# Merging two dilated attention outputs: the factors by transposed statistics and a spreading transfer in place of small copies and TensorE transposes

## The chip, the cores and the metric

The kernel runs on one core of one Trainium2 chip. The metric is the device time of one execution in microseconds (us). Beside the time of an execution stands its span in the profile, from the first to the last instruction.

Engine names are those of the profile: PE is TensorE's matmul (PEld its weight load), DVE is VectorE, ACT is ScalarE, POOL is GpSimd, SP is SyncE, whose queue issues nearly all transfers.

## The reference

One encoder block on 1024 positions of width 1024: a normalised and modulated input is projected to q, k, v of two attentions (A dilated, B neighbourhood) and to gates; both attentions are projected, gated, added; a ConvFFN follows. The change is in attention A. It has 8 heads of width 64 and three patterns of the same q, k, v, whose results are merged by their softmax denominators:

```python
DIL_PATTERNS = ((128, 1), (512, 4), (2048, 16))

def mixture_of_dilations(q, k, v, rel_bias):
    outs, lses = [], []
    for window, dilation in DIL_PATTERNS:
        o, lse = dilated_window_attention(q, k, v, rel_bias, window, dilation)
        outs.append(o)
        lses.append(lse)                       # lse = m + log(l), the row maximum and the sum of exponentials
    w = jax.nn.softmax(jnp.stack(lses, axis=0), axis=0)
    return jnp.einsum('gbsh,gbshd->bshd', w, jnp.stack(outs, axis=0))
```

## The kernel before

Everything is kept transposed: channels on the partitions, positions along the free dimension, in an order in which the four residues modulo 4 stand in blocks of 256 ("r"). Products are made of three float32r matmuls each (L84 to L86: high by high, high by low, low by high), with operands split into a high and a low part.

**The mixers' stage.** From about 157 to 655 us the attentions run in 101 slots, written out by hand. In each slot some steps of attention are interleaved with `fill` steps, which are the remaining projections (L84 to L86, or L365): one step is one k of such a product, a job has sixteen. The order of PE, DVE and ACT in this stage is the order of the program text (`manual_schedule`). POOL and SP are not in that list: a planner with a timeline of its own places their instructions, and once placed, each queue runs strictly in order on the chip. The projections' weights are loaded by `w_load` (L65), two buffers deep, and split by ACT (L638, high part) and POOL (L639, low part) one job ahead; a load waits until the split of the job before has freed its buffer.

**A dilated head** takes 16 score tiles: in slots s0 to s0+3 the "far" ones (patterns 2 and 3 together, one residue r at a time), in s0+4 to s0+7 the "near" ones (pattern 1, blocks b of 128 positions). DVE adds the bias and takes the negative maximum, ACT takes the exponential and its sum (`softmax`, L579). Both go into a column of the tile `st`: 128 partitions, heads i of the pair, statistic (near maximum, near sum, far maximum, far sum), 8 columns. Two slots later PE transposes the probabilities into a PSUM tile T (L703 far, L749 near), ACT and DVE split it (L588, L589), one slot later PE multiplies by v (L715, L766), and ACT and DVE bring the result to the tiles u1 (near) and u23 (far): 128 partitions = two heads of 64 channels, 1024 positions, not yet divided by anything. PSUM holds two T tiles.

**The merge** is made for each of the four pairs of heads (`DilPair`, s0 = 16 times the pair). Near and far statistics lie in different orders over the partitions: near has partition = (r, j) and column = block b, far has partition = (q, j) with 32 j, and column = 2r + g. Before the change:

- `exchange` (L799): sixteen DVE copies of 32 partitions a pair, in slots s0+13 to s0+16, bring the far statistics into near order (xs).
- `factors` (s0+16) and `shares` (s0+17): a few DVE operations on 128 x 16 and one exponential on ACT give the two factors, near and far, for every position.
- `give` (L825): sixteen DVE copies a pair bring the far factor back into far order (fx).
- `spread` (L830, POOL): one factor column is repeated over 64 columns, for four blocks and two heads at once: fw, 128 x 512. `weigh` (L838, L840): PE transposes fw in four pieces into a T tile, which so holds the factor on all 64 channel partitions of its head, and DVE multiplies 512 columns of u by it. Four times a pair: near and far, two halves.
- `merge` (L847, POOL): u23 plus u1, reordered; the result goes to DRAM (L848, `oa`) and is read in the stage behind the mixers.

After the four pairs come the eight heads of attention B in slots 64 to 100. The last pair's merge falls into their first slots.

Of the kernel before, what the change touches and what calls it, by code (L numbers as in the profile page):

```python
# [17 lines left out]
S = 1024  # L18
# [11 lines left out]
def hybrid_encoder(tc, xT, c, w_ada, small, w_in, p1_bias, p23_bias, na_bias, ln2_mult, ident, w_br, w_out,  # L30
# [198 lines left out]

    vb_c = dram.tile([S, 512], FT, name="vbc")  # L230
    g_scr = dram.tile([16, 128, S], FT, name="gs")
    o_scr = [dram.tile([4, 128, S], FT, name=n) for n in ("oa", "ob")]
    v_scr = dram.tile([S + 9 * 128, 512], FT, name="v")
    va_s, va_b = v_scr[:S], v_scr[S:].rearrange("(j p) n -> j p n", j=9)
# [413 lines left out]
    class DilHead:  # L648
# [32 lines left out]
        def far_scores(self, r):  # L681
            qs, ks, kl, qb = qks[self.pr]
            ensure(qk_marks[self.pr])
            i, st = self.i, self.st()
            s = ps_l.tile([128, 512], FT, name="S")
            P = self.P[r] = sm_pool.tile([128, 2, 256], FT, name="P", bufs=5)
            for g in range(2):
                d = s[:, 256 * g:256 * g + 256]
                qc = slice(256 * r + 128 * g, 256 * r + 128 * g + 128)
                kc = slice(256 * r, 256 * r + 256)  # L690
                pe.matmul(d, qs[i][:, qc], ks[i][:, kc], start=True, stop=False)
                pe.matmul(d, qs[i][:, qc], kl[i][:, kc], start=False, stop=True)  # L692
            for g in range(2):
                d = s[:, 256 * g:256 * g + 256]
                e = 2 * r + g
                softmax(d, self.bt[:, 640 - 128 * g:896 - 128 * g], P[:, g], st[:, i, 2, e:e + 1], st[:, i, 3, e:e + 1])

        def far_turn(self, r):
            P = self.P.pop(r)
# [20 lines left out]
        def near_scores(self, n):  # L720
            qs, ks, kl, qb = qks[self.pr]
            ensure(qk_marks[self.pr])
            i, st = self.i, self.st()
            s = ps_l.tile([128, 512], FT, name="S")
            P = sm_pool.tile([128, 2, 256], FT, name="P", bufs=5)
            for x_ in range(2):
                b = 2 * n + x_
                t0, t1 = block_chunks(b)[0]
                d = s[:, 256 * x_:256 * x_ + 256]
                mid = t0 is not None and t1 is not None  # L730
                for dd, *keys in [(d, t0, 2)] if mid else [(d[:, 0:128], t0), (d[:, 128:256], t1)]:
                    pe.matmul(dd, qb[i][:, 128 * b:128 * b + 128], window(ks[i], *keys), start=True, stop=False)
                    pe.matmul(dd, qb[i][:, 128 * b:128 * b + 128], window(kl[i], *keys), start=False, stop=True)
            for x_ in range(2):
                b = 2 * n + x_
                off = block_chunks(b)[1]
                softmax(s[:, 256 * x_:256 * x_ + 256], self.bt[:, off:off + 256], P[:, x_], st[:, i, 0, b:b + 1],
                        st[:, i, 1, b:b + 1])
                self.P["near", b] = P[:, x_]

        def near_turn(self, js):
# [31 lines left out]
    class DilPair:  # L773
        def __init__(self, pr):
            self.pr, s0 = pr, 16 * pr
            at(s0, "first", self.begin) if pr else self.begin()
            for i in range(2):
                DilHead(self, pr, i, s0 + 8 * i, lambda: self.u, lambda: self.st)
            for r in range(4):
                at(s0 + 13 + r, "first", self.exchange, r)  # L780
                at(s0 + 18 + r, "first", self.give, r)
            at(s0 + 16, "last", self.factors)
            at(s0 + 17, "last", self.shares)
            for n, (g, z) in enumerate(((0, 0), (0, 1), (1, 0), (1, 1))):
                s = s0 + 18 + n + g
                at(s, "last", self.spread, g, z)
                at(s + 2, "W", self.weigh, g, z)
            at(s0 + 25, "first", self.merge)

        def begin(self):  # L790
            self.u = [at_pool.tile([128, S], FT, name=n) for n in ("u1", "u23")]
            self.st = sm_pool.tile([128, 2, 4, 8], FT, name="st")
            self.fw = {}

        def exchange(self, r):
            if r == 0:
                self.xs = at_pool.tile([128, 2, 2, 8], FT, name="xs")
            for q in range(4):
                dve.tensor_copy(self.xs[32 * r:32 * r + 32, :, :, q:8:4],  # L799
                                self.st[32 * q:32 * q + 32, :, 2:4, 2 * r:2 * r + 2])  # L800

        def factors(self):
            st, xs = self.st, self.xs
            fa = at_pool.tile([128, 2, 2, 8], FT, name="fa")
            fb = at_pool.tile([128, 2, 2, 8], FT, name="fb", bufs=1)
            fl = at_pool.tile([128, 2, 8], FT, name="fl", bufs=1)
            dve.tensor_tensor(fl, st[:, :, 0], xs[:, :, 0], OP.min)
            dve.tensor_tensor(fa[:, 0], fl, st[:, :, 0], OP.subtract)
            dve.tensor_tensor(fa[:, 1], fl, xs[:, :, 0], OP.subtract)
            act.activation(fa, fa, AF.Exp)  # L810
            self.fa, self.fb, self.fl = fa, fb, fl

        def shares(self):
            st, xs, fa, fb, fl = self.st, self.xs, self.fa, self.fb, self.fl
            dve.tensor_tensor(fb[:, 0], fa[:, 0], st[:, :, 1], OP.mult)
            dve.tensor_tensor(fb[:, 1], fa[:, 1], xs[:, :, 1], OP.mult)
            dve.tensor_tensor(fl, fb[:, 0], fb[:, 1], OP.add)
            dve.reciprocal(fl, fl)
            for g in range(2):
                dve.tensor_tensor(fa[:, g], fa[:, g], fl, OP.mult)  # L820
            self.fac = [fa[:, 0], at_pool.tile([128, 2, 8], FT, name="fx")]

        def give(self, r):
            for q in range(4):
                dve.tensor_copy(self.fac[1][32 * q:32 * q + 32, :, 2 * r:2 * r + 2],  # L825
                                self.fa[32 * r:32 * r + 32, 1, :, q:8:4])

        def spread(self, g, z):
            fw = self.fw[g, z] = at_pool.tile([128, 4, 2, 64], FT, name="fw")
            pool.tensor_scalar(fw, self.fac[g][:, :, 4 * z:4 * z + 4].rearrange("p i b -> p b i")  # L830
                               .rearrange("p b (i o) -> p b i o", o=1).to_broadcast([128, 4, 2, 64]), 1.0, None, OP.mult)

        def weigh(self, g, z):
            fw = self.fw.pop((g, z))
            ensure(self.done)
            pt = ps_a.tile([128, 512], FT, name="T")
            for b in range(4):
                pe.transpose(pt[:, 128 * b:128 * b + 128], fw[:, b], idt)  # L838
            dst = self.u[g][:, 512 * z:512 * z + 512]
            return lambda: dve.tensor_tensor(dst, dst, pt, OP.mult)  # L840

        def merge(self):
            u = self.u
# [882 lines left out]
```

## Time and profile before

| | |
|---|---|
| time, median of 3 runs | 1537.97 us (1537.17 to 1539.8) |
| profiled execution: time | 1539.41 us |
| profiled execution: span | 1537.3 us |
| mean granted TensorE clock | 0.988 |
| PE busy over the span | 1499.0 us (98%) |
| DVE, ACT, POOL busy | 996.0, 770.4, 775.8 us (65%, 50%, 50%) |
| DMA: moved, share of 16 engines (queue q1) | 205.24 MB in all, 41.1% |

How its lines are read: a group's line names the source line, the engine, the operation, the tiles written and read, the shape and the count; then its busy time in us and the mean ns of one; then the idle time of the engine just before them and what ended it. A line of the timeline names the start in us, the duration in us, the engine, the line, and in brackets the idle time before it. A line of the table by stage has the stretch, then for PE, PEld, DVE, ACT and POOL the busy time with the number of instructions, the granted clock, the DMA share and GB/s. A line of DMA issues ends with the median us from issue to landing. A line of the waits has the total us waited, how often, and the longest. Matmuls are pipelined and their ends are modelled, so the distance from start to start says more than the durations.

### The profile page before, as it was taken

The page shows a single profiled execution, that of the slowest core. Times are in us where ns is not written, and L with a number is a line of the kernel's source. Part 1 is how long each engine was busy: PE and PEld are TensorE (multiplying, and loading weights), DVE is VectorE, ACT ScalarE, POOL GpSimd, SP SyncE. Part 2 cuts the span into 40 slices and gives each one's busy share as a digit, 9 for nine tenths or more (in the row PEclk, how much of TensorE's full clock was granted, in tenths as well). Part 3 has the DMA queues.
Part 4 walks back from the last instruction along what each step waited for, and adds up shares of the span by engine and source line. Part 5 has one row for each costly group of instructions (what it writes and reads, how often), then busy time and mean ns, then how long its engine had stood idle before and what let it go on. Part 6 is the DMA issues. An engine that isn't in the chain of part 4 may idle for free. (4 is left out here: it accounts for less than half of the span.)

```text
span 1537.3 us, 21792 instructions
## 1 busy us (share of the span) xinstructions
PE 1499.0 (98%) x7740; PEld 1270.1 (83%) x7740; DVE 996.0 (65%) x1892; ACT 770.4 (50%) x1437; POOL 775.8 (50%) x640
## 2 busy tenths in 40 slices
PE   8999999999999999999999899999999998999997
PEld 7988888889798998878888677888888887878787
DVE  6675357575656655645525888876666667786765
ACT  4331566666656566643345454444444447475542
POOL 1021344443335444512267668776777765779721
PEclk8999999999999999999999999999999999999999
DMA  9567333333625456577644112222222224523323
GB/s 352 187 240 258 94 106 81 108 91 104 185 82 153 127 140 171 154 241 232 213 141 154 62 62 96 90 82 83 82 82 85 87 79 162 193 75 124 117 55 110
DMA packets 112436, 205.24 MB, mean 134 GB/s; under 512 B 40484, under 2 KB 53156, under 8 KB 112292
## 3 DMA queue, kind: packets, MB, share of 16 engines
q1 hardware_dynamic: 112056, 203.59, 41.1%
q8 instruction: 61, 1.00, 0.3%
q14 instruction: 47, 0.39, 0.1%
q10 hardware_dynamic: 272, 0.26, 0.1%
HBM read 158.73 MB, written 42.47 MB: 131 GB/s over the span
## 5 line engine op out<-in xcount | busy, mean ns | idle before, releaser
L61 POOL TENSOR_TENSOR wlo<-wraw,whi 128x512 fp32r<-128x512 f32 (+1 forms) x96 | 118.3, 1253 | 172.9 <-ACT whi L57 139.1
L84 PE MATMUL pj<-h,whi 128*128 128x512 f32 x448 | 187.7, 419 | 1.8 <-ACT h L207 1.4
L85 PE MATMUL pj<-h,whi 128*128 128x512 f32 x448 | 177.8, 397 | 1.6 <-DVE h L209 1.6
L86 PE MATMUL pj<-h,wlo 128*128 128x512 f32 x448 | 177.2, 396 | 0.0
L61 POOL TENSOR_TENSOR wsl<-big,wsh 128x512 fp32r<-128x512 f32 (+1 forms) x90 | 123.6, 1395 | 47.7 <-ACT wsh L57 47.7
L639 POOL TENSOR_TENSOR wlo<-wraw,whi 128x512 fp32r<-128x512 f32 x58 | 74.9, 1301 | 117.2 <-ACT whi L638 117.2
L589 DVE TENSOR_TENSOR tl<-T,th 128x512 fp32r<-128x512 f32 (+3 forms) x120 | 77.1, 653 | 72.9 <-ACT th L588 71.4
L1384 DVE SCALAR_TENSOR_TENSOR big<-wc,sm,big 128x256 f32<-128x256 f32 (+1 forms) x132 | 106.9, 859 | 16.1 <-ACT big L1378 15.9
L581 ACT ACTIVATE P<-P,st 128x256 f32<-128x256 f32 x128 | 64.1, 502 | 95.9 <-DVE st L580 95.9
L86 PEld LDWEIGHTS pj<-h,wlo 128*128 128x128 f32 x448 | 85.0, 190 | 18.9
L84 PEld LDWEIGHTS pj<-h,whi 128*128 128x128 f32 x448 | 85.6, 191 | 13.6 <-ACT h L207 1.9
L85 PEld LDWEIGHTS pj<-h,whi 128*128 128x128 f32 x448 | 85.6, 191 | 13.2 <-DVE h L209 3.0
L57 ACT ACTIVATE whi<-wraw 128x1024 fp32r<-128x1024 f32 (+2 forms) x52 | 50.7, 975 | 73.0 <-PE pj L85 27.6
L1384 DVE SCALAR_TENSOR_TENSOR big<-pj,sm,big 128x512 f32<-128x512 f32 x132 | 67.0, 563 | 17.6 <-ACT big L1378 17.6
L61 POOL TENSOR_TENSOR wsl<-wraw,wsh 128x384 fp32r<-128x384 f32 (+1 forms) x46 | 54.4, 1204 | 44.6 <-ACT wsh L57 44.4
L910 POOL TENSOR_SCALAR P<-P,stb 128x288 f32<-128x288 f32 (+1 forms) x32 | 40.2, 1257 | 72.1 <-DVE stb L907 64.7
L588 ACT ACTIVATE th<-T 128x512 fp32r<-128x512 f32 (+3 forms) x120 | 65.6, 566 | 20.3 <-PE T L919 14.0
L1378 ACT ACTIVATE big<-wc,sm 128x512 f32<-128x512 f32 x44 | 35.8, 815 | 69.3 <-DVE wc L1202 42.3
L57 ACT ACTIVATE wsh<-big 128x1024 fp32r<-128x1024 f32 (+1 forms) x45 | 44.7, 998 | 46.2 <-POOL big L1154 32.6
L547 POOL TENSOR_TENSOR vv<-vv 128x512 fp32r<-128x512 f32 (+1 forms) x40 | 42.0, 1069 | 48.5 <-ACT vv L546 48.5
L1410 ACT ACTIVATE big<-big 128x1024 f32<-128x1024 f32 x22 | 23.3, 1060 | 80.0 <-DVE big L1384 80.0
L580 DVE CUSTOM_DVE_ANT_0 P<-S,bias 128x256 f32<-128x256 f32 x128 | 48.9, 419 | 21.3 <-PE S L692 17.1
(395 smaller groups left out, 4799.3 us busy)
## 6 DMA issues: line engine op xcount, KB each, us to landing
wraw<-w_in SPq DMA_DIRECT2D x34, 512.0 KB, 4.2
wada<-w_ada SPq DMA_DIRECT2D x31, 512.0 KB, 7.9
big<-w_up SPq DMA_DIRECT2D x22, 512.0 KB, 5.4
wraw<-w_up SPq DMA_DIRECT2D x22, 512.0 KB, 3.7
as<-big SPq DMA_DIRECT2D x22, 512.0 KB, 3.0
big<-as SPq DMA_DIRECT2D x22, 512.0 KB, 8.0
wraw<-w_down SPq DMA_DIRECT2D x24, 384.0 KB, 3.8
gs<-gs SPq DMA_DIRECT2D x32, 256.0 KB, 2.9
```

The source lines that it names most:

```text
L57: act.activation(hi, raw, AF.Copy)
L61: lo_eng.tensor_tensor(lo[:, i:i + step], raw[:, i:i + step], f(hi)[:, i:i + step], OP.subtract)
L84: pe.matmul(psum, whi[:, k0 + k], mhi, start=k == 0, stop=False)
L85: pe.matmul(psum, whi[:, k0 + k], mlo, start=False, stop=False)
L86: pe.matmul(psum, wlo[:, k0 + k], mhi, start=False, stop=k == n - 1)
L547: pool.tensor_tensor(lo[:m, cs_], f(lo[:m, cs_]), f(vv[:m, cs_, 0:64]), OP.subtract)
L580: dve.tensor_tensor_reduce(pp, d, bias, -1.0, BIG, OP.add, OP.min, mi)
L581: act.activation(pp, pp, AF.Exp, bias=mi, scale=-1.0, accum_out=li)
L588: act.activation(th[:m, :n], pt[:m, :n], AF.Copy)
L589: dve.tensor_tensor(tl[:m, :n], pt[:m, :n], f(th)[:m, :n], OP.subtract)
L639: pool.tensor_tensor(lo[:, i:i + n], raw[:, i:i + n], f(hi)[:, i:i + n], OP.subtract)
L1384: dve.scalar_tensor_tensor(y[:, dst], src, wt, y[:, dst], OP.mult, OP.add)
```

## The change

The statistics are turned once by PE (`turn`: 128 x 64 into 64 x 128, in slot s0+16), copied out of PSUM by DVE, and stored in DRAM (`st_scr`). Nine transfers on SP bring them back to a tile fs of 64 partitions x 4 statistics x 32, in which near and far agree: one for the far ones, eight for the near ones (two heads, four residues). `factors` (now s0+19) and `shares` (s0+20) work on this layout. The two factors go to DRAM (`f_scr`) in nine transfers, each in the order of its own u tile. For each of the four quarters a transfer reads 512 factors of each of the two heads and repeats them over the 64 partitions of the head (fb, one buffer of 128 x 512), and POOL multiplies u by it. `merge` is called in slot s0+23 in place of s0+25. `exchange`, `give`, `spread` and `weigh` are gone.

```diff
--- before.py
+++ after.py
@@ -229,6 +229,8 @@
 
     vb_c = dram.tile([S, 512], FT, name="vbc")
     g_scr = dram.tile([16, 128, S], FT, name="gs")
+    st_scr = dram.tile([4, 64, 128], FT, name="sts")
+    f_scr = dram.tile([4, 2, 2, S], FT, name="fcs")
     o_scr = [dram.tile([4, 128, S], FT, name=n) for n in ("oa", "ob")]
     v_scr = dram.tile([S + 9 * 128, 512], FT, name="v")
     va_s, va_b = v_scr[:S], v_scr[S:].rearrange("(j p) n -> j p n", j=9)
@@ -693,7 +695,7 @@
             for g in range(2):
                 d = s[:, 256 * g:256 * g + 256]
                 e = 2 * r + g
-                softmax(d, self.bt[:, 640 - 128 * g:896 - 128 * g], P[:, g], st[:, i, 2, e:e + 1], st[:, i, 3, e:e + 1])
+                softmax(d, self.bt[:, 640 - 128 * g:896 - 128 * g], P[:, g], st[:, 2, i, e:e + 1], st[:, 3, i, e:e + 1])
 
         def far_turn(self, r):
             P = self.P.pop(r)
@@ -734,8 +736,8 @@
             for x_ in range(2):
                 b = 2 * n + x_
                 off = block_chunks(b)[1]
-                softmax(s[:, 256 * x_:256 * x_ + 256], self.bt[:, off:off + 256], P[:, x_], st[:, i, 0, b:b + 1],
-                        st[:, i, 1, b:b + 1])
+                softmax(s[:, 256 * x_:256 * x_ + 256], self.bt[:, off:off + 256], P[:, x_], st[:, 0, i, b:b + 1],
+                        st[:, 1, i, b:b + 1])
                 self.P["near", b] = P[:, x_]
 
         def near_turn(self, js):
@@ -776,68 +778,62 @@
             at(s0, "first", self.begin) if pr else self.begin()
             for i in range(2):
                 DilHead(self, pr, i, s0 + 8 * i, lambda: self.u, lambda: self.st)
-            for r in range(4):
-                at(s0 + 13 + r, "first", self.exchange, r)
-                at(s0 + 18 + r, "first", self.give, r)
-            at(s0 + 16, "last", self.factors)
-            at(s0 + 17, "last", self.shares)
-            for n, (g, z) in enumerate(((0, 0), (0, 1), (1, 0), (1, 1))):
-                s = s0 + 18 + n + g
-                at(s, "last", self.spread, g, z)
-                at(s + 2, "W", self.weigh, g, z)
-            at(s0 + 25, "first", self.merge)
+            at(s0 + 16, "T", self.turn)
+            at(s0 + 19, "last", self.factors)
+            at(s0 + 20, "last", self.shares)
+            at(s0 + 23, "first", self.merge)
 
         def begin(self):
             self.u = [at_pool.tile([128, S], FT, name=n) for n in ("u1", "u23")]
-            self.st = sm_pool.tile([128, 2, 4, 8], FT, name="st")
-            self.fw = {}
-
-        def exchange(self, r):
-            if r == 0:
-                self.xs = at_pool.tile([128, 2, 2, 8], FT, name="xs")
-            for q in range(4):
-                dve.tensor_copy(self.xs[32 * r:32 * r + 32, :, :, q:8:4],
-                                self.st[32 * q:32 * q + 32, :, 2:4, 2 * r:2 * r + 2])
+            self.st = sm_pool.tile([128, 4, 2, 8], FT, name="st")
+
+        def turn(self):
+            pt = ps_a.tile([128, 512], FT, name="T")
+            pe.transpose(pt[:64, :128], self.st.rearrange("p s i b -> p (s i b)"), idt)
+            return lambda: self.rows(pt)
+
+        def rows(self, pt):
+            rows = at_pool.tile([64, 128], FT, name="rows", bufs=1)
+            dve.tensor_copy(rows, pt[:64, :128])
+            sp.dma_start(st_scr[self.pr], rows)
+            self.fs = at_pool.tile([64, 4, 32], FT, name="fs", bufs=1)
+            sp.dma_start(self.fs[:, 2:4], st_scr[self.pr][32:64].rearrange("(s x) (q j) -> (x q) s j", s=2, j=32))
+            near = st_scr[self.pr][0:32].rearrange("(s i b) (r j) -> i r b s j", s=2, i=2, r=4)
+            for i in range(2):
+                for r in range(4):
+                    sp.dma_start(self.fs[32 * i + 8 * r:32 * i + 8 * r + 8, 0:2], near[i, r])
 
         def factors(self):
-            st, xs = self.st, self.xs
-            fa = at_pool.tile([128, 2, 2, 8], FT, name="fa")
-            fb = at_pool.tile([128, 2, 2, 8], FT, name="fb", bufs=1)
-            fl = at_pool.tile([128, 2, 8], FT, name="fl", bufs=1)
-            dve.tensor_tensor(fl, st[:, :, 0], xs[:, :, 0], OP.min)
-            dve.tensor_tensor(fa[:, 0], fl, st[:, :, 0], OP.subtract)
-            dve.tensor_tensor(fa[:, 1], fl, xs[:, :, 0], OP.subtract)
+            fs = self.fs
+            self.fa = fa = at_pool.tile([64, 2, 32], FT, name="fa", bufs=1)
+            self.fl = fl = at_pool.tile([64, 32], FT, name="fl", bufs=1)
+            dve.tensor_tensor(fl, fs[:, 0], fs[:, 2], OP.min)
+            for g in range(2):
+                dve.tensor_tensor(fa[:, g], fl, fs[:, 2 * g], OP.subtract)
             act.activation(fa, fa, AF.Exp)
-            self.fa, self.fb, self.fl = fa, fb, fl
 
         def shares(self):
-            st, xs, fa, fb, fl = self.st, self.xs, self.fa, self.fb, self.fl
-            dve.tensor_tensor(fb[:, 0], fa[:, 0], st[:, :, 1], OP.mult)
-            dve.tensor_tensor(fb[:, 1], fa[:, 1], xs[:, :, 1], OP.mult)
-            dve.tensor_tensor(fl, fb[:, 0], fb[:, 1], OP.add)
+            fs, fa, fl = self.fs, self.fa, self.fl
+            for g in range(2):
+                dve.tensor_tensor(fs[:, 2 * g], fa[:, g], fs[:, 2 * g + 1], OP.mult)
+            dve.tensor_tensor(fl, fs[:, 0], fs[:, 2], OP.add)
             dve.reciprocal(fl, fl)
             for g in range(2):
                 dve.tensor_tensor(fa[:, g], fa[:, g], fl, OP.mult)
-            self.fac = [fa[:, 0], at_pool.tile([128, 2, 8], FT, name="fx")]
-
-        def give(self, r):
-            for q in range(4):
-                dve.tensor_copy(self.fac[1][32 * q:32 * q + 32, :, 2 * r:2 * r + 2],
-                                self.fa[32 * r:32 * r + 32, 1, :, q:8:4])
-
-        def spread(self, g, z):
-            fw = self.fw[g, z] = at_pool.tile([128, 4, 2, 64], FT, name="fw")
-            pool.tensor_scalar(fw, self.fac[g][:, :, 4 * z:4 * z + 4].rearrange("p i b -> p b i")
-                               .rearrange("p b (i o) -> p b i o", o=1).to_broadcast([128, 4, 2, 64]), 1.0, None, OP.mult)
-
-        def weigh(self, g, z):
-            fw = self.fw.pop((g, z))
+            to = f_scr[self.pr]
+            sp.dma_start(to[1].rearrange("i (x j) -> (i x) j", j=32), fa[:, 1])
+            near = to[0].rearrange("i (b r j) -> i r b j", b=8, r=4)
+            for i in range(2):
+                for r in range(4):
+                    sp.dma_start(near[i, r], fa[32 * i + 8 * r:32 * i + 8 * r + 8, 0])
             ensure(self.done)
-            pt = ps_a.tile([128, 512], FT, name="T")
-            for b in range(4):
-                pe.transpose(pt[:, 128 * b:128 * b + 128], fw[:, b], idt)
-            dst = self.u[g][:, 512 * z:512 * z + 512]
-            return lambda: dve.tensor_tensor(dst, dst, pt, OP.mult)
+            for g in (1, 0):
+                for z in range(2):
+                    fb = at_pool.tile([128, 512], FT, name="fb", bufs=1)
+                    sp.dma_start(fb, to[g][:, 512 * z:512 * z + 512].rearrange("i (o n) -> i o n", o=1)
+                                 .to_broadcast([2, 64, 512]))
+                    dst = self.u[g][:, 512 * z:512 * z + 512]
+                    pool.tensor_tensor(dst, dst, fb, OP.mult)
 
         def merge(self):
             u = self.u
```

## The prediction

> **What bounds the kernel now.** I read the page first, then the stage in which the merge runs (205 to 540 us), and then the order of instructions around one merge.
>
> ```profile
> span 1537.3 us, 21792 instructions
> PE 1499.0 (98%) x7740; PEld 1270.1 (83%) x7740; DVE 996.0 (65%) x1892; ACT 770.4 (50%) x1437; POOL 775.8 (50%) x640
> ```
> ```profile
> 205.00:540.00 335.00, 330.60 (x2046) 289.39 (x2045) 211.03 (x625) 203.10 (x502) 143.05 (x121) 1.00 0.39 113
> ```
>
> The last line is the table by stage: PE is busy for 330.6 of 335 us at full clock, DVE for 63% of it, POOL for 43%. A busy PE need not be a full one, so I read the starts of its instructions around two of the sixteen weighings (L838).
>
> ```profile
> 246.75 0.39 PE L86 MATMUL pj<-h,wlo 128*128 128x512 f32 x1
> 246.99 0.60 PE L838 MATMUL T<-idt,fw 128*128 128x128 f32 x4
> 247.34 0.48 PE L84 MATMUL pj<-h,whi 128*128 128x512 f32 x1
> 247.66 0.40 PE L85 MATMUL pj<-h,whi 128*128 128x512 f32 x1
> 247.89 0.40 PE L86 MATMUL pj<-h,wlo 128*128 128x512 f32 x1
> 248.41 0.66 PE L703 MATMUL T<-idt,P 128*128 128x128 f32 x4
> ...
> 409.91 0.40 PE L86 MATMUL pj<-h,wlo 128*128 128x512 f32 x1
> 412.01 0.66 PE L749 MATMUL T<-idt,P 128*128 128x128 f32 x4 [1.70 <-DVE tl L589]
> ```
>
> A 128x512 product follows the one before it by 0.23 us (247.66 to 247.89), with no hole: PE is full, and every instruction taken off it shortens the stage. The T groups at 248.41 and 412.01 are exceptions: each comes later than 0.23 us behind its L86, stands close behind a weighing, which had taken one of the two T buffers, and had to wait for a split to free one.
>
> **The change part by part.** *PE.* Four transposes of a weighing hold the next product up by 0.35 us (246.99 to 247.34), and the product behind them starts its successor after 0.32 in place of 0.23 us, so one weighing costs 0.35 + 0.09 = 0.44 us. Sixteen: 7.0 us, all on the path. Added are four transposes, one a pair, each behind a group of four that is there anyway: 0.35/4 = 0.09 us, 0.35 us together. Net 6.65 us.
>
> *T buffers.* Seven groups of transposes (first 248.41, last 412.01) start later than the 0.23 us behind their L86, each within a dozen matmuls of an L838. The first is 0.52 - 0.23 = 0.29 us late, the last 2.10 - 0.23 = 1.87, the other five between 0.03 and 0.32; together 3.17 us. Without the weighing's tile these waits go. The new transpose takes a second T tile in slot 16 only: its copy follows the split that ends at 227.63 (rows below), and the next group that needs a buffer comes a slot later, at about 230, so it brings no wait. Bound: 0 to 3.2 us gained; I take 3.15, because each late group has its L838. PE sum: -9.8 us.
>
> *DVE and POOL* (the groups by line):
>
> ```profile
> L825 DVE COPY fx<-fa 32x4 f32<-32x4 f32 x64 | 18.8, 294 | 1.0
> ...
> L799 DVE COPY xs<-st 32x8 f32<-32x8 f32 x64 | 11.4, 178 | 1.0
> L840 DVE TENSOR_TENSOR u<-u,T 128x512 f32<-128x512 f32 x16 | 10.9, 682 | 6.8 <-PE T L838 6.8
> ```
> ```profile
> L830 POOL TENSOR_SCALAR fw<-fa 128x512 f32<-128x512 f32 x8 | 11.8, 1493 | 16.5 <-DVE fa L820 16.5
> L847 POOL TENSOR_TENSOR u<-u,u 128x512 f32<-128x512 f32 x8 | 10.2, 1304 | 3.5 <-DVE u L840 1.8 <-DVE stb L907 1.7
> ```
>
> DVE loses 11.4 + 18.8 + 10.9 = 41 us and gains four copies of some 0.2 us; POOL exchanges sixteen spreads of 1.49 us (eight from fa, as shown, eight from fx) for sixteen products, priced like L847 at 1.30. Both are off the path: counted at nothing.
>
> *The chain through DRAM*, 23 transfers a pair, all on SP. The first half must reach DVE before `factors`, three slots after `turn`. Single rows picked from the timeline of each engine and from the list of transfers:
>
> ```profile
> 225.13 0.19 ACT L581 ACTIVATION_READ_ACCUMULATOR P<-P,st 128x1 f32 x1
> 225.68 0.60 PE L749 MATMUL T<-idt,P 128*128 128x128 f32 x4
> 226.94 0.69 DVE L589 TENSOR_TENSOR tl<-T,th 128x512 fp32r<-128x512 f32 x1 [1.42 <-ACT th L588]
> 228.76 0.64 DVE L807 TENSOR_TENSOR fl<-st,xs 128x16 f32<-128x16 f32 x1
> 230.96 0.23 PE L766 MATMUL O<-th,vv 128*128 128x128 f32 x1
> 270.81 0.33 SPq L848 DMA_DIRECT2D oa<-u  x1
> 341.65 0.33 SPq L848 DMA_DIRECT2D oa<-u  x1
> 237.20 0.57 SPq L482 DMA_DIRECT2D vv<-v  x1
> xs<-x SPq DMA_DIRECT2D x16, 256.0 KB, 2.2
> ```
>
> The two L848 are one pair of heads apart: 70.84 us, 4.43 us a slot. The last statistics are there at 225.32; the new transpose comes behind the group at 225.68, with 0.7 us to spare, so PE does not wait. DVE copies at 227.8, the store lands 0.35 + 2.2 us later (230.4), nine loads at 0.57 us of issue are out by 235.5, and land by 237.7 at the same 2.2. `factors` in slot 19 comes three slots after L807: 242.0. Spare: 4.3 us, if SP is free. The exponential waits behind it on ACT and everything behind that on DVE; how much lateness PE forgives is seen in the split that ends at 227.63 and is wanted at 230.96: 3.3 us.
>
> The second half starts with `shares` at 246.5 (slot 20, four slots after L807): 1.3 us of DVE, nine stores at 0.57 us (253), and then four times a load of 256 KB into the single buffer fb and a product of 1.30 us on POOL, each load waiting on SP for the product before. What such a load takes decides. Rows for 256 KB to 128 partitions, and for the DMA work as a whole:
>
> ```profile
> q1 hardware_dynamic: 112056, 203.59, 41.1%
> gs<-gs SPq DMA_DIRECT2D x32, 256.0 KB, 2.9
> 115.20 3.03 SPq L371 DMA_DIRECT2D v<-v  x4
> 119.50 0.91 SPq L65 DMA_DIRECT2D wraw<-w_in  x2
> wraw<-w_in SPq DMA_DIRECT2D x2, 512.0 KB, 12.9
> wraw<-w_in SPq DMA_DIRECT2D x34, 512.0 KB, 4.2
> ```
>
> 41.1% of 16 x 1537.3 us for 203.59 MB is 49.7 us of one engine per MB, so 13 us for 256 KB: 0.8 us on sixteen engines, which leaves 2.1 us of fixed time in gs. The source here is an access of two rows, each repeated 64 times: its slowest dimension has size 2. The nearest row is L371, four transfers of seven blocks of 64 KB (1.84 MB, 91 us of engine time). On sixteen engines they would be through in 5.7 us and the two weight loads behind them would land as usual; they landed in 12.9 us, not 4.2, at about 132.5. On seven engines L371 ends at 115.2 + 2.1 + 13.0 = 130.3, which fits. So by the row that is nearest, this load runs on two engines: 2.1 + 6.5 = 8.6 us; the other bound is 2.9.
>
> [...]
>
> With 8.6 us a round is 0.35 + 8.6 + 1.3 = 10.25 us, and the four end at 253 + 41 = 294, the store of the merge some 3 us later; now it leaves at 270.81. Nobody needs it: the array that it fills is read only in the stage behind the mixers, and the u buffers are written again by the pair after next in slot 36 (228.76 + 20 x 4.43 = 317). The load's length is thus hidden as long as POOL and SP have other work placed ahead of the waits. Cost taken: 0, for this cover; without it the first rival.
>
> *Sum.* Against the profiled execution of 1539.41 us (span 1537.3, 2.1 us around it): 1539.4 - 9.8 = 1529.6. The median of the runs shown, 1537.97, is 1.4 us below that execution, so 1528.2.
>
> **The rivals.**
>
> ```profile
> 266.99 1.29 POOL L639 TENSOR_TENSOR wlo<-wraw,whi 128x512 fp32r<-128x512 f32 x1
> 270.74 1.29 POOL L639 TENSOR_TENSOR wlo<-wraw,whi 128x512 fp32r<-128x512 f32 x1
> 272.06 0.33 SPq L65 DMA_DIRECT2D wraw<-w_in  x1
> wraw<-w_in SPq DMA_DIRECT2D x1, 512.0 KB, 4.4
> 279.78 0.62 ACT L638 ACTIVATE whi<-wraw 128x512 fp32r<-128x512 f32 x1
> SPq L65 <- POOL wlo L639: 53.9, 14, 12.6
> ```
>
> *POOL stands in its queue for the narrow loads, and the weight splits stand behind it.* POOL and SP are ordered by the planner's clock, not by hand. If that clock takes the load for an ordinary one (2.9 us), it sets a product into POOL's queue 5.7 us too early in each round, and by the third round everything behind is 17 us late. Behind it are the two halves of L639: they free the buffer for the load at 272.06, which lands at 276.5 and is split at 279.78, with 3.3 us to spare. 17 - 3.3, less the 3.3 us that PE forgives, is 10.5 us a pair, 42 us in four: -9.8 + 42 gives 1570. It decides from the point where a round runs 3 us longer than planned (9 us in three; 9 - 6.6 = 2.4 us a pair eats the gain). For it: the serial single buffer, and the 8.6 us. Against it: POOL is 57% idle, and in the stage now PE hardly ever waits for an order that came out badly. [...] Chance 0.25, spread from 1538 to 1570, about half of it below 1556.
>
> *The statistics come late to `factors`.* The longest wait that SP now stands out for a weight buffer is 12.6 us (last row above). If the store or one of the nine loads is queued behind such a wait, they land 12.6 - 4.3 = 8.3 us late, 3.3 of them forgiven: 5 us a pair, 20 in all, net +10: 1548. It decides from 4.3 + 3.3 + 2.4 = 10 us of delay on SP. For it: 23 more transfers take 13 us of SP's issue time a pair; against: the planner can put them ahead of a wait that it foresees. Chance 0.13.
>
> *Only part of it arrives*: some small lateness of either kind, 1 to 2.5 us a pair, leaves between -6 and +1 us, around 1535. Chance 0.14, half of it within 3 us of now.
>
> **How the numbers follow.** The forecast, 1528.2, has 0.48; its own range is 1524 to 1533 (the T waits not gained, 1531.3; a few DVE waits more, 1525). A measurement of this kernel can tell about 0.2%, 3.1 us, from no change. Faster: 0.48 + 0.07 = 0.55. Same: 0.07. Slower: 0.25 + 0.13 = 0.38. The range of 1524 to 1556 leaves out the upper half of the first rival and little at the low end, some 0.17.
>
> **What would show it.** Right: no L838, PE's start-to-start around slots 18 to 24 back at 0.23 us, no T wait behind a split there, the load of fb landing near 8.6 us, `oa` leaving some 25 us later. Wrong in the first way: POOL products with a long idle before them ended by the load of fb, L639 late, ACT's split waiting for the weight load, holes on PE once a pair. Wrong in the second: the minimum of `factors` on DVE ended by the load of fs. If fb lands in about 3 us, the two engines were wrong but the sum stands. If PE shows no hole and the time is still not lower by 6 us, the reading that PE is full there was wrong.

## The result, and the profile after

| | before | after |
|---|---|---|
| time, median of 4 runs each | 1538.88 us | 1558.16 us (1557.41 to 1561.6) |
| ratio, 95% interval | | 1.013 [1.0114, 1.0147] |
| profiled execution: span | 1537.3 us | 1556.3 us |
| its mean granted clock | 0.988 | 0.980 |

The change made the kernel 1.3% slower. The forecast of 1528.2 us was wrong in sign; the time lies 2 us above the upper end of the range, and inside the span that the first rival gave (1538 to 1570).

The page of the changed kernel, the lines that answer to those of before:

```profile
span 1556.3 us, 21656 instructions
PE 1502.8 (97%) x7680; PEld 1272.3 (82%) x7680; DVE 953.3 (61%) x1752; ACT 772.2 (50%) x1437; POOL 770.2 (49%) x640
PEclk8999999999999899999999999999999999999999
```

DVE lost 42.7 us (41 were worked out), POOL 5.6. PE has fewer instructions and yet a longer busy time, which a row of stages explains (PE, PEld, DVE, ACT, POOL, then clock, DMA share, GB/s):

```profile
205.00:540.00 335.00, 315.26 (x1882) 276.21 (x1881) 158.61 (x458) 191.99 (x480) 130.79 (x115) 0.97 0.42 119
500.00:535.00 35.00, 24.81 (x142) 23.11 (x142) 12.57 (x27) 9.60 (x24) 18.38 (x16) 0.80 0.43 135
```

In the stage of the merges PE was busy for 330.6 of 335 us; now it is for 315.3, with 164 instructions fewer done in the same time (60 of them are transposes that the change takes away), and the clock is 0.97 in place of 1.00. The end of the last pair (500 to 535 us) is worst: 24.8 of 35 us, at clock 0.80. What PE waits for in the mixers' stage is mostly POOL, and next ACT (total us, times, longest):

```profile
PE O L928 <- POOL vv L549: 4.7, 2, 3.2
PE pj L86 <- POOL wlo L641: 3.4, 1, 3.4
PE T L915 <- POOL P L906: 2.9, 1, 2.9
PE pj L367 <- POOL wlo L641: 2.6, 1, 2.6
PE T L792 <- ACT P L583: 2.4, 2, 1.2
```

In the kernel before, the same view has six rows, 6.5 us together, and POOL is in none of them; two of them are

```profile
PE T L749 <- DVE tl L589: 1.9, 2, 1.7
PE O L766 <- DVE tl L589: 0.9, 1, 0.9
```

And POOL itself stands for the new load. In the changed kernel the load is L833, the product L836, the addition of the merge L843, the low half of the weights L641 (L639 before), the split of v L549, the normalisation of attention B L906:

```profile
POOL u L836 <- DMA fb<-fcs: 94.0, 15, 12.6
```

The last pair shows how one becomes the other. SP's loads, then POOL's instructions, then PE's (lines left out are marked ...):

```profile
506.60 0.50 SPq L833 DMA_DIRECT2D fb<-fcs  x1
515.53 0.51 SPq L833 DMA_DIRECT2D fb<-fcs  x1
```
```profile
514.24 1.26 POOL L836 TENSOR_TENSOR u<-u,fb 128x512 f32<-128x512 f32 x1 [5.22 <-DMA fb<-fcs]
515.48 1.24 POOL L906 TENSOR_SCALAR P<-P,stb 128x384 f32<-128x384 f32 x1
516.69 0.72 POOL L549 TENSOR_TENSOR vv<-vv 96x256 fp32r<-96x256 f32 x1
...
523.86 1.26 POOL L836 TENSOR_TENSOR u<-u,fb 128x512 f32<-128x512 f32 x1 [3.27 <-DMA fb<-fcs]
525.20 1.26 POOL L843 TENSOR_TENSOR u<-u,u 128x512 f32<-128x512 f32 x1
526.43 1.24 POOL L906 TENSOR_SCALAR P<-P,stb 128x384 f32<-128x384 f32 x1
```
```profile
517.46 0.39 PE L928 MATMUL O<-th,vv 96*128 96x256 f32 x1 [3.24 <-POOL vv L549]
...
527.73 0.89 PE L915 MATMUL T<-idt,P 128*128 128x128 f32 x4 [2.93 <-POOL P L906]
```

The load goes out at 506.60 and its product starts at 514.24, 7.6 us later; the next takes 8.3 (515.53 to 523.86). The packet records of the trace show why: the load that goes out at 506.60 moves as 128 packets of 2 KB, from 507.90 to 513.69, two at a time for nearly all of it, each 0.08 us long as a rule. In `wide` (below) a load of the same 128 packets, issued at 486.36, passes from 487.59 to 489.74, with up to 15 at once. The normalisation and the v split of attention B, which need nothing of the merge, stand behind the products on POOL, and PE waits for both. In the third pair and once in the last (507.85) it waits in the same way for a low half of the weights, L641: 3.4 and 2.6 us, the two rows above.

In the first two pairs the way is another one. Here the store of another tensor is caught, gs, the projected gates (SP, ACT, PE):

```profile
280.63 0.54 SPq L833 DMA_DIRECT2D fb<-fcs  x1
281.26 0.42 SPq L976 DMA_DIRECT2D gs<-gs  x1
```
```profile
289.51 0.60 ACT L975 ACTIVATE gs<-pj 128x512 f32<-128x512 f32 x1 [4.47 <-DMA gs<-gs]
```
```profile
291.52 0.33 PE L768 MATMUL O<-th,vv 128*128 128x128 f32 x1 [0.83 <-ACT th L590]
297.11 0.30 PE L792 MATMUL T<-idt,st 128*64 128x128 f32 x1 [1.20 <-ACT P L583]
```

The gs store was issued right behind a load of fb, and its buffer came free for ACT only about when fb had landed, after 8.3 us, where gs took 2.9 before. The packets show the two side by side: 256 of 2 KB, 128 for each transfer, up to 19 at once at first, but from 283.1 to 288.9 two at a time in the main. The product that needs fb starts at 288.78, and ACT goes on at 289.51. ACT stood for 4.47 us, its split th came late to PE, and so did the last exponentials, behind which the new transpose L792 waits.

### The profile page after: what moved, and what is told of

The parts are those of the page before. It is cut to its first block, busy times and chain, and to the rows that moved or that the text cites. A ratio compares the mean times of both kernels' runs of the same rounds, so it can differ in the third digit from the quotient of the medians.

```text
span 1556.3 us, 21656 instructions
## 1 busy us (share of the span) xinstructions
PE 1502.8 (97%) x7680; PEld 1272.3 (82%) x7680; DVE 953.3 (61%) x1752; ACT 772.2 (50%) x1437; POOL 770.2 (49%) x640
## 5 line engine op out<-in xcount | busy, mean ns | idle before, releaser
L86 PE MATMUL pj<-h,wlo 128*128 128x512 f32 x448 | 177.5, 396 | 3.4 <-POOL wlo L641 3.4
L641 POOL TENSOR_TENSOR wlo<-wraw,whi 128x512 fp32r<-128x512 f32 x58 | 74.5, 1297 | 85.9 <-ACT whi L640 84.2
L1380 DVE SCALAR_TENSOR_TENSOR big<-wc,sm,big 128x256 f32<-128x256 f32 (+1 forms) x132 | 103.2, 830 | 16.8 <-ACT big L1374 16.6
L86 PEld LDWEIGHTS pj<-h,wlo 128*128 128x128 f32 x448 | 85.3, 190 | 22.6 <-POOL wlo L641 3.8
L906 POOL TENSOR_SCALAR P<-P,stb 128x288 f32<-128x288 f32 (+1 forms) x32 | 39.7, 1241 | 77.4 <-DVE stb L903 59.2
L836 POOL TENSOR_TENSOR u<-u,fb 128x512 f32<-128x512 f32 x16 | 20.5, 1284 | 98.8 <-DMA fb<-fcs 94.0
L899 ACT ACTIVATE P<-P,stb 128x288 f32<-128x288 f32 (+1 forms) x64 | 36.4, 569 | 50.9 <-DVE stb L897 50.8
```

Source lines behind the costliest of these rows:

```text
L86: pe.matmul(psum, wlo[:, k0 + k], mhi, start=False, stop=k == n - 1)
L641: pool.tensor_tensor(lo[:, i:i + n], raw[:, i:i + n], f(hi)[:, i:i + n], OP.subtract)
L1380: dve.scalar_tensor_tensor(y[:, dst], src, wt, y[:, dst], OP.mult, OP.add)
```

## The experiments

Each stands against the kernel before, run on the same chip. Diffs of `wide`, `two_buffers`, `no_loads`, `wide_last`, `narrow_halves`, `dve_products` and `wide_dve` are against the changed kernel, the others against the one before. "Stage" is the mixers' stage of the profiled execution, from the start of the first far scores to the start of the last output on PE (501.8 us before, 519.7 after).

| | time us | before us | ratio, 95% | stage us |
|---|---|---|---|---|
| wide | 1531.62 | 1539.22 | 0.9957 [0.994, 0.9974] | 492.8 |
| two_buffers | 1566.81 | 1539.22 | 1.0179 [1.0164, 1.0194] | 526.9 |
| no_loads | 1536.73 | 1539.22 | 0.999 [0.9971, 1.0008] | 497.0 |
| no_weigh | 1545.47 | 1539.22 | 1.004 [1.003, 1.005] | 506.9 |
| wide_last | 1541.15 | 1539.4 | 1.0016 [1.0004, 1.0028] | 504.1 |
| narrow_halves | 1569.96 | 1539.4 | 1.0196 [1.0174, 1.0217] | 533.9 |
| dve_products | 1529.87 | 1539.4 | 0.9941 [0.9923, 0.9959] | 491.7 |
| bare | 1529.85 | 1539.4 | 0.9937 [0.9914, 0.996] | 490.5 |
| wide_dve | 1529.29 | 1539.27 | 0.9937 [0.9918, 0.9956] | 491.7 |
| no_give | 1529.23 | 1539.27 | 0.9935 [0.9914, 0.9956] | 490.8 |

**wide: the same bytes with 64 in the outermost place.**

```diff
-                    sp.dma_start(fb, to[g][:, 512 * z:512 * z + 512].rearrange("i (o n) -> i o n", o=1)
-                                 .to_broadcast([2, 64, 512]))
+                    for i in range(2):
+                        sp.dma_start(fb[64 * i:64 * i + 64],
+                                     to[g][i:i + 1, 512 * z:512 * z + 512].to_broadcast([64, 512]))
```

> The changed kernel, but each load of fb is issued as two transfers of 64 partitions whose outermost size is 64 on both sides; bytes, buffer and order of the program text stay. Theory A (a load confined to two engines keeps POOL standing in its queue, and the weight splits, the v splits and the normalisations behind it come late): from issue to product a load takes 3 to 5 us in place of 8.3 (median over the sixteen), POOL's idle time ended by fb falls from 94 us to under 40, PE's holes of over 1.5 us in the mixers' stage and the half-clock stretches behind them go, and the time falls from 1558 to 1531 to 1536. Theory B (the single buffer and the chain product-load-product in two in-order queues do it at any width): the loads get shorter, the time stays above 1548.

1531.62 us: 0.43% faster than before, and some 27 us faster than the change. Nothing else was changed by hand, and POOL's instructions come in the same order through the first two pairs. From the third pair on the order differs from the changed kernel's in 13 of 640 places: in `wide` some splits stand ahead of a product that they follow in the changed kernel. `narrow_halves` settles whether that order or the width made the gain. From the first issue to the product a load now takes 3.5 to 6.1 us, median 4.1. The tile fb and PE's stages:

```profile
L837 POOL TENSOR_TENSOR u<-u,fb x16: 1273/1295/1303, 254.5 to 497.9; 128x512 f32<-128x512 f32 x16
...
  DMA fb<-fcs: 20.6, 10
```
```profile
205.00:540.00 335.00, 331.29 (x2030) 291.60 (x2029) 175.07 (x499) 210.27 (x519) 145.86 (x127) 1.00 0.47 132
```

POOL's wait for fb fell from 94.0 to 20.6 us, PE is full again at clock 1.00, and ACT has no wait for gs at all (15.3 us in the changed kernel, none before).

**two_buffers: the narrow loads two deep.**

```diff
-            rows = at_pool.tile([64, 128], FT, name="rows", bufs=1)
+            rows = at_pool.tile([128, 512], FT, name="fb", bufs=2)[:64, :128]
...
-                    fb = at_pool.tile([128, 512], FT, name="fb", bufs=1)
+                    fb = at_pool.tile([128, 512], FT, name="fb", bufs=2)
```

> The changed kernel with two fb buffers in place of one; the loads stay narrow (the copy of the turned statistics takes one of the two for want of space). Theory A (the narrow load): two loads share the same two engines, so four products still need some 25 us of transport; little is won, 1550 to 1558. Theory B (the single buffer, and SP standing behind each product): SP no longer stands for a product, each second load is hidden, and the time falls to 1532 to 1542.

1566.81 us, worse than one buffer and above the end of either expectation. Two loads at once took 7.8 to 14.65 us each from issue to product. So two loads side by side did not each keep the 8.2 of one; that they share the same engines is the author's reading, which no record shows. POOL waited 80.2 us for fb in place of 94.0, and PE paid more:

```profile
PE pj L86 <- POOL wlo L641: 16.8, 4, 7.4
```

So a second buffer did not help. (The small tile of the turned statistics shares the two buffers here, which the changed kernel's does not, and POOL's order differs from the changed kernel's in 28 of 640 places.)

**no_loads: POOL fills fb with ones in place of the loads,** so the factors don't reach u.

```diff
-                    sp.dma_start(fb, to[g][:, 512 * z:512 * z + 512].rearrange("i (o n) -> i o n", o=1)
-                                 .to_broadcast([2, 64, 512]))
+                    pool.memset(fb, 1.0)
```

> The changed kernel without the sixteen loads of fb: POOL fills the buffer with ones and multiplies by it, so the two outputs are added unweighted; statistics, factors and their way to DRAM stay. Theory A and B alike: with no load to stand for, POOL and SP keep step; 1529 to 1535. Theory C (the way of the statistics through DRAM, or the turn that waits for the last exponential, costs the time): stays above 1548.

1536.73 us, 21 below the change, but above the expected end of 1535. The loss goes with the loads; it stays 5 us above `wide`, and the two intervals just touch. The sixteen fills lengthen POOL's list by 0.53 us each; whether that is what is left was not tried. Its trace has one half-clock stretch of 3.4 us (408.4) that `wide` has not.

**no_weigh: the kernel before without its weighings** (u stays unweighed; everything else is made).

```diff
-            pt = ps_a.tile([128, 512], FT, name="T")
-            for b in range(4):
-                pe.transpose(pt[:, 128 * b:128 * b + 128], fw[:, b], idt)
-            dst = self.u[g][:, 512 * z:512 * z + 512]
-            return lambda: dve.tensor_tensor(dst, dst, pt, OP.mult)
+            return lambda: None
```

> The kernel before without its sixteen weighings: no transposes of fw, no product with u on DVE; exchange, give and spread stay, so the two outputs are added unweighted. It prices what the change takes off PE. The prediction's sum (7.0 us of transposes and 3.2 us of waits for a T buffer): 1538.9 - 10.2 = 1528 to 1530. If PE has slack there, or later stages take it back: above 1535.

A miss: 1545.47 us, 6 slower than with the weighings. The sum of the prediction would be refuted if nothing else had changed. But the addition of the merge moved forward on POOL, and DVE's small copies of `give` (L825, 0.16 us as a rule) met it:

```profile
L825 DVE COPY fx<-fa x64: 147/163/3016, 233.3 to 482.8; 32x4 f32<-32x4 f32 x64
```
```profile
240.34 1.70 DVE L825 COPY fx<-fa 32x4 f32<-32x4 f32 x4
240.39 1.29 POOL L843 TENSOR_TENSOR u<-u,u 128x512 f32<-128x512 f32 x1 [5.04 <-DVE u L624]
...
242.08 0.69 DVE L589 TENSOR_TENSOR tl<-T,th 128x512 fp32r<-128x512 f32 x1
...
242.82 0.39 PE L715 MATMUL O<-tl,vv 128*128 128x256 f32 x1 [0.84 <-DVE tl L589]
```

Four copies took 1.70 us in place of 0.65, and the split behind them made PE wait. That was a reading made after the miss; `no_give` puts it to the test.

**wide_last: wide loads in the last pair alone** (`if self.pr == 3:` the two transfers of `wide`, else the narrow one).

> The changed kernel with the loads of fb made wide in the last pair only; the first three pairs keep the narrow loads. It tells where the 27 us lie by which the changed kernel is behind the wide one (1558.2 to 1531.6). By the traces the changed kernel is 10.8 us behind the wide one when attention B's first scores begin, and 26.9 at the end of the stage. Theory A (each pair loses what its own narrow loads hold up, and the last most, since POOL's normalisations and v splits of attention B stand behind its products): 1539 to 1545. Rival (the last pair alone does it): 1531 to 1535. Rival (the loss is even): 1550 to 1553.

1541.15 us. Against `wide` the three narrow pairs cost 9.1 us (1.0016 less 0.9957, of 1539), and the narrow last pair some 17.5 (after is 1.3% above before, this one 0.16%). The traces divide it by pair: counted from the start of the stage, the turn on PE of the second, third and fourth pair comes 2.8, 5.6 and 10.9 us later in the changed kernel than in `wide`, and the last output 26.9 us later. So the pairs cost 2.8, 2.8, 5.3 and 16.0 us. One load, several prices: in the last pair attention B's work shares POOL's queue.

**narrow_halves: two transfers again, but split by columns, so that 2 stays outermost.**

```diff
-                    sp.dma_start(fb, to[g][:, 512 * z:512 * z + 512].rearrange("i (o n) -> i o n", o=1)
-                                 .to_broadcast([2, 64, 512]))
+                    for c in (0, 256):
+                        sp.dma_start(fb[:, c:c + 256],
+                                     to[g][:, 512 * z + c:512 * z + c + 256].rearrange("i (o n) -> i o n", o=1)
+                                     .to_broadcast([2, 64, 256]))
```

> The changed kernel with each load of fb issued as two transfers, like the wide kernel, but cut along the columns: each keeps an outermost size of 2, with pieces of 1 KB. A control for the wide kernel: if its gain comes from the width, this one stays at 1555 to 1566; if it comes from issuing two transfers (another order by the planner, two semaphores), it falls below 1545.

1569.96 us, above the expected 1566. As many transfers as in `wide`, of the same size, POOL's 640 instructions in the very order of `wide`, and some 37 us slower (1.0196 less 0.9957, of 1539). So it is neither the number of transfers nor the order on POOL that helped `wide`, but the size of the outermost dimension. (The pieces are 1 KB here and 2 KB in `wide` and in the changed kernel; what part the smaller pieces have in the 10 us above the changed kernel, 1.0196 less 1.013, was not tried.) The way over gs grew with it (ACT's wait for gs 28.7 us, and on PE):

```profile
PE O L768 <- ACT th L590: 13.0, 4, 4.1
```

**dve_products: the narrow loads as they were, the products on DVE, placed by hand** three slots apart (two in the last pair), each followed by the next load.

```diff
-            at(s0 + 23, "first", self.merge)
+            for n in ((24, 27, 30, 33), (22, 24, 26, 28))[pr == 3]:
+                at(s0 + n, "last", self.product)
+            at(s0 + (34, 29)[pr == 3], "first", self.merge)
...
+        def product(self):
+            _, g, z = self.jobs.pop(0)
+            dst = self.u[g][:, 512 * z:512 * z + 512]
+            dve.tensor_tensor(dst, dst, self.fb, OP.mult)
+            if self.jobs:
+                self.fetch()
```

> The changed kernel with its narrow loads, but the sixteen products on DVE in place of POOL, put by hand three slots apart (two in the last pair), so that each load has landed when DVE comes to its product; merge is called later accordingly. Theory A (the loss comes from POOL standing in its queue in front of the splits and normalisations, not from the transfers as such): 1530 to 1540, with POOL's idle time for fb gone. Rival (two engines busy with broadcasts, or SP standing for the product, hold up the weight loads as well): above 1548.

1529.87 us: the narrow load costs next to nothing when almost nobody stands for it. The run changes two things, the engine and the place of the products, and does not say which of them is enough. The tile fb (on DVE 0.69 us, where POOL takes 1.29):

```profile
L847 DVE TENSOR_TENSOR u<-u,fb x16: 683/689/1186, 264.8 to 526.8; 128x512 f32<-128x512 f32 x16
...
  DMA fb<-fcs: 2.6, 1
```

**bare: the kernel before with no factors at all** (no exchange, factors, shares, give, spread or weighing; the merge only adds).

```diff
-            for r in range(4):
-                at(s0 + 13 + r, "first", self.exchange, r)
-                at(s0 + 18 + r, "first", self.give, r)
-            at(s0 + 16, "last", self.factors)
-            at(s0 + 17, "last", self.shares)
-            for n, (g, z) in enumerate(((0, 0), (0, 1), (1, 0), (1, 1))):
-                s = s0 + 18 + n + g
-                at(s, "last", self.spread, g, z)
-                at(s + 2, "W", self.weigh, g, z)
+            at(s0 + 24, "first", lambda: ensure(self.done))
```

> The kernel before without exchange, factors, shares, give, spread and weigh: the two outputs are added unweighted, nothing else is changed. It prices the whole of the old merge arithmetic without any new transfer, and without the small copies that met POOL in the kernel without weighings. The prediction's sum for PE (7.0 us of transposes and 3.2 us of T waits): 1538.9 - 10.2 = 1528 to 1530, or a little less if the small copies held DVE up. If PE has slack there: above 1535.

1529.85 us. All that the old way of weighing cost is 9.6 us, so no other way can win more than about that; `dve_products` has won all of it within the intervals.

**wide_dve: both, wide loads and products on DVE** (the two edits together).

> The kernel with the products on DVE, put by hand, and the wide loads as well. Theory A (a load costs only where an in-order queue with other work stands for it): with the products three slots apart the width no longer matters, so the time stays at that of the narrow loads on DVE, 1528 to 1532. Rival (the broadcasts also slow other transfers down): 2 to 4 us below it, 1525 to 1527.

1529.29 us, not to be told from `dve_products`. Away from POOL the width of the load no longer matters.

**no_give: `no_weigh`, and without the copies of `give` too** (the far factor is read in its near order).

```diff
-                at(s0 + 18 + r, "first", self.give, r)
...
-            self.fac = [fa[:, 0], at_pool.tile([128, 2, 8], FT, name="fx")]
+            self.fac = [fa[:, 0], fa[:, 1]]
...
+            return lambda: None
```

> The kernel without weighings, and without the sixteen copies of give a pair as well (spread reads the far factor in the wrong order; the outputs are added unweighted). In the kernel without weighings three copies a pair of give last until a POOL product ends, 1.2 us and once 3.0 us in place of 0.16, and PE has holes behind them. If these meetings are why that kernel was slower than the kernel before: 1528 to 1533. If something else in it was (the spreads, the earlier merge on POOL): above 1538.

1529.23 us, 16 below `no_weigh`. The copies were what kept its gain away, and taking the weighings from PE is worth what the sum said, within the interval.

## Why the prediction was wrong, and where it was right

*The PE sum held.* -9.8 us was worked out for the weighings, the turns and the T buffers. `dve_products` gives -9.5 and `wide_dve` -10.0. `bare` and `no_give`, which have no turns, give -9.6 and -10.0 against -10.2. Each has an interval of about 3 us to either side; `wide` has -7.6 (from -9.2 to -4.0). That PE is full in this stage, and that an instruction taken off it shortens the stage, was right. The part for the T buffers was taken too large: the 1.7 us before the T group at 412.01 went, but without the weighings PE waits longer for a split elsewhere, 1.8 us in place of the 0.9 shown above:

```profile
PE O L766 <- DVE tl L589: 1.8, 1, 1.8
```

That line is from `bare`; `no_give` has the same, and `wide` and `dve_products` have it as L768. The runs can't tell 1 us in the total. (The kernel before has eight late groups, not seven; their sum is still 3.2.)

*The load's length held.* 8.6 us and a round of 10.25 were worked out from the seven blocks of L371; from issue to product it was 7.6 to 9.3 us, median 8.2, and the loads of the last pair follow one another by 9 us, somewhat less than the round. That the load runs on two engines was the author's estimate, and no run shows it: the records have no engine numbers. What the packets show is that the load at 506.60, with 2 outermost, moved two at a time for 5.1 of its 5.8 us, and that the one at 486.36 in `wide`, with 64 outermost, moved up to 15.

*The chain through DRAM held.* `factors` was to run at 242.0, with the statistics there ahead of it. Its first reading of fs runs at 241.9, and the trace lists no idle time of DVE before it:

```profile
L810 DVE TENSOR_TENSOR fl<-fs x4: 177/179/180, 241.9 to 474.3; 64x32 f32<-64x32 f32 x4
```

So the second rival did not happen. The 0.7 us to spare for the turn held in `wide`; in the changed kernel PE waited for it in two pairs, 1.2 us each (L792 above), since ACT was already late.

*The step that failed* is "Cost taken: 0, for this cover". The condition stood in the prediction: as long as POOL and SP have other work placed ahead of the waits. It was not given. POOL stood 94.0 us for fb, and weight splits, v splits and normalisations stood behind its products. The order did not price the load's length: `narrow_halves` and `wide` have the same one. The cost taken as 0 was some 29 us, by `dve_products`. The deadline that the prediction looked at, the oa store that nobody needs for long, was indeed kept, and did not matter. What mattered were the consumers of the work queued behind the product.

*The first rival had the mechanism, with the wrong size and mostly other victims.* It priced only the weight split, 10.5 us in every pair, 42 in all, on top of the sum. Measured against `dve_products`, the loss is 29 us (1.013 less 0.9941, of 1539). Against `wide` it is 2.8 us in each of the first two pairs, which lose through gs and ACT, 5.3 in the third, which loses through L641 (3.4 us), and 16.0 in the last, where v and the normalisation of attention B are the victims, and L641 again (2.6 us). Nor did the split come late by the way that the rival named, a weight load held up by a full buffer: ACT's waits in this stage have no weight load among them; PE waited for L641 itself. The rival had not seen that other transfers on SP could be slowed by the load. That the time lies inside its span is in part luck, since the span was made of four equal pairs.

*Where the 27 us between the change and `wide` are.* PE's waits in the stage, taking the rows of 1 us and more, sum to 22.2 us in the changed kernel (nine rows, of which five stand above) and to 4.0 in `wide`, whose rows are

```profile
PE O L768 <- DVE tl L591: 1.8, 1, 1.8
PE O L929 <- DVE tl L591: 1.2, 4, 0.5
PE O L929 <- ACT th L590: 1.0, 1, 1.0
```

That is 18 us. The rest is the clock: 0.97 over 335 us is 20 us at 0.5, which, had PE worked through them, would be 10 us of work, an estimate from above. The waits and the clock overlap in part, so the split is not exact.

*Shown and only argued.* Shown by runs: a wide load (`wide` against `narrow_halves`), or the product on another engine at another place (`dve_products`, `wide_dve`), is each enough to undo the loss. Shown by the packets: the narrow load at 506.60 moves two at a time in the main, and so do, taken together, the load at 280.63 and the gs store behind it (4.9 of the 5.8 us from 283.1 to 288.9). Argued: that these are the same two engines; the records have no engine numbers. Open: whether products on POOL, placed later by hand, would have done as well; why `no_loads` is 5 us above `wide`, and whether the 2 us between `wide` and `wide_dve` are there at all, since their intervals overlap.

## What to carry to other kernels

Before an instruction that waits for a transfer is put on an engine whose queue is in order, ask what is queued behind it, and who waits for that (here POOL stood 94.0 us for fb, and PE waited for what POOL did behind it); "its result is not needed for long" is only half of the question. The broadcast from DRAM took 8.2 us from issue to product with 2 in the outermost place and 4.1 with 64; where the slow one stayed, a consumer placed by hand where the data have landed waited 2.6 us for it in all (`dve_products`). What a step costs at all is best bounded by a run without it (`bare`), and where such a run comes out the wrong way, look for what moved into the gap before giving up the sum.

## What the runs showed of the hardware

**The clock fell after short holes.** In the changed kernel the granted clock is 0.5 for stretches of 3.4 or 6.8 us (412.0, 432.4, 507.5, 517.8 and 528.0, 20.5 us together) soon after a hole on PE of 1.8 to 3.4 us. Inside such a stretch the same four products last 1.16 in place of 0.61 us:

```profile
520.00:524.00 4.00, 3.35 (x15) 3.35 (x16) 0.02 (x1) 0.65 (x2) 0.73 (x2) 0.50 0.41 108
```
```profile
522.42 1.16 PE L367 MATMUL pj<-h,whi 128*128 128x256 f32 x4
...
532.39 0.61 PE L367 MATMUL pj<-h,whi 128*128 128x256 f32 x4
```

Two holes of 1.2 us brought none in the changed kernel, and one of 1.8 us brought one there and none in `wide`, so the length of a hole alone did not decide. Within each trace the changes of the clock lie on one grid of 3.41 us. Cut along this grid into cells, the changed kernel (150 to 680 us) has five cells at full clock that were followed by one at half clock; PE was idle for 52.6, 65.9, 75.0, 86.0 and 90.7% of them, and for 47.1% of the idlest cell that was not so followed. In the kernel before it was idle for 53.9% of the one cell that was followed so, and for 49.8% of the idlest that was not. Counted over the twelve traces, every cell at full clock with 53.9% or more (there are 16) was followed by one at half clock, no cell below 51% was, and of the nine between, five were. What makes the clock fall is not shown. The L641 that L86 waited for at 431.59 was so paid for twice: by a hole of 3.35 us on PE, and by 3.4 us at half clock from 432.4 on.

**Some small DVE copies lasted until POOL's instruction ended.** A copy of 32x4 values takes 0.16 us, and took up to 3.0 us in `no_weigh` where POOL's instructions ran beside it. There one of the four copies shown above started at 240.51 and ended at 241.70, just behind the end of POOL's addition (240.39 + 1.29). The kernel before has 11 such copies of over 0.5 us, 9.8 us together; each ended 0.01 to 0.03 us behind the end of an instruction of POOL. Six others ran wholly inside one of POOL's spreads (L830, 1.49 us) and took 0.15 to 0.16 us, so not every meeting was slow; what tells them apart is not shown. `no_weigh` has 12 of over 0.5 us, 14.2 us together. So it is their place more than their number that cost.
